# Five blocks of projection columns of an encoder layer, 2560 in all, as seven products of halves instead of eight

## The chip, the cores and the metric

One core of a Trainium2 chip runs the kernel; every time is in device microseconds (us) of that core. PE is TensorE (matmuls), DVE VectorE, ACT ScalarE, POOL GpSimd, and SP SyncE, whose queue issues the DMAs. Lower is better. Before: median 1946.49 us over 3 runs (1945.42 to 1948.09).

## The reference

One layer on a sequence of 1024 tokens, 2048 wide. A normed input is multiplied with one combined weight matrix; its columns are cut into the inputs and gates of four mixers, each gated mixer output is one 512 wide quarter of `y`, and a second matrix brings `y` back.

```python
h = rms_norm(x, norm_g) @ w_in                    # [1024, 2048] @ [2048, 6408]
(a_u, a_v, a_z, b_q, b_k, b_v, b_iq, b_ik, b_iw, b_z,
 c_q, c_kv, c_kr, c_z, d_q, d_k, d_v, d_z) = split_cols(h, IN_SIZES)
y_a = gmlp_mixer(a_u, a_v, ...) * silu(a_z)       # gelu of u and v, spatial mixing
y_b = dsa_mixer(b_q, ..., b_ik, b_iw) * silu(b_z) # index scores, top 256 keys, attention
y_c = mla_mixer(c_q, c_kv, c_kr, ...) * silu(c_z) # attention over low-rank keys
y_d = band_mixer(d_q, d_k, d_v, ...) * silu(d_z)  # attention over nine chunks
x = x + concat([y_a, y_b, y_c, y_d]) @ w_out
```

## The kernel before

**Arithmetic.** Every float32 operand of a large product is cut into a high and a low part (`xh`, `xl`; `wh`, `wl`), and a product is three matmuls: high by high, high by low, low by high. Parts of weights are made by an ACT cast (`wh`, L419) and a POOL subtract (`wl`, L420); parts of activations by an ACT cast and a DVE subtract (`split`, L242 and L243). The normed input, transposed, stays in SBUF as 16 tiles `xh`, `xl` of 128x2048 (tags "th" and "tl", eight each).

**Input projection.** A pass takes 256 columns and all 2048 rows, in eight weight loads of 256 rows. `project` moves 256 weight columns against stationary tokens (matmuls of 256 columns); `project_t` moves 512 tokens against stationary weights (512 columns) and is used where the result is wanted transposed: for the index queries (2 passes), the gates B_Z, D_Z, C_Z, A_Z and the input A_U (2 passes each, ten of twelve). Four PSUM banks are filled in a pass (`banks4`); each is evacuated to a tile of `htile`, a ring of five SBUF tiles called `hs`, and stored to DRAM from there. B_Q, D_K and D_Q are normed on the way: ACT copies the bank (L478) and squares it (L235), DVE norms (L236 to L239), SP stores (L500).

**Order of the work.** PE's program is in the order in which the code issues it. The mixers are generators: a clock in `Driver` counts modelled PE time, `pump` in the projections' loops lets every mixer that is due issue its next piece, so that their short matmuls stand between those of the projections. The other engines are list-scheduled, with `hi_prio` pieces ahead; each engine and SP's one queue then runs its list strictly in order. The top-256 selection is a loop of 31 counting steps: DVE counts five of six row blocks (L700), POOL the sixth (`tq`, L697), ACT sums that (L698). Before, the order of the projections is IQ, B_Q, B_Z, D_V, D_Z, C_Q/C_KV, D_K, D_Q, C_Z, A_V, A_U, A_Z; gates are stored in `sz_d`, and the mixers load them (`z`) and multiply.

**Output.** `w_out` is multiplied as eight units of 512 columns (n=0: groups 1 and 3, n=1: groups 2 and 0), each a product of two by two halves done as seven products (`out_unit`: the Winograd form of Strassen's scheme). `prepare` loads `y` and makes its seven operand halves (A11, S2, S1, S3, A12, A22, S4) in the "th" and "tl" tiles. Results go to PSUM banks X, Y (tag "pp", four), Z ("sc") and are added to `xr`, the residual's tile (L1340 from PSUM, L1348 the first product, from SBUF).

Of the kernel before, what the change touches and what calls it, by code (L numbers as in the profile page):

```python
# [9 lines left out]
F32 = mybir.dt.float32  # L10
# [8 lines left out]
P = 128  # L19
# [116 lines left out]
def build(tc, i, out, dbg=None):  # L136
# [16 lines left out]
    sz_d = dram("sz_d", [2048, SEQ])  # L153
# [237 lines left out]
    hctx, yctx = ExitStack(), ExitStack()  # L391
# [88 lines left out]

    def project_gate(c0, g0):
        for c in range(2):
            def evac(j, hf, ps):
                h = htile()
                with hi_prio():
                    A.activation(h, ps, AF.Tanh, scale=0.5)
                    V.scalar_tensor_tensor(h, h, 1.0, ps, op0=ALU.add, op1=ALU.mult)
                r0 = g0 + 256 * c + P * j
                S.dma_start(sz_d[r0:r0 + P, 512 * hf:512 * hf + 512], h)
            project_t(c0 + 256 * c, evac)  # L490
# [117 lines left out]

    def gate(pl, row, c0, n):
        z = pl.tile([P, n], F32, tag="z", name="z", bufs=1)  # L610
        S.dma_start(z, sz_d[row:row + P, c0:c0 + n])
        return z
# [117 lines left out]
    def b_attention(ap, maskb):  # L730
# [9 lines left out]
        def unit(idx, hp_, b):  # L740
# [26 lines left out]
            if b % 2:  # L767
                po = state["po"]
                row = GB + P * hp_
                z = gate(ap, row, P * (b - 1), 256)  # L770
# [9 lines left out]
                V.tensor_tensor(y, y, z, op=ALU.mult)  # L780
# [23 lines left out]
    def d_attention(ap):  # L804
# [4 lines left out]
        def unit(idx, h, m):  # L809
# [31 lines left out]
            if m % 2:  # L841
# [3 lines left out]
                z = ap.tile([P, 512], F32, tag="z", name="z", bufs=1)  # L845
                S.dma_start(z[r0:r0 + 64], sz_d[row:row + 64, c0:c0 + 512])
# [6 lines left out]
                V.tensor_tensor(y[r0:r0 + 64], y[r0:r0 + 64], z[r0:r0 + 64], op=ALU.mult)  # L853
# [150 lines left out]
    def c_attention(ap):  # L1004
# [11 lines left out]
        def unit(idx, h, b):  # L1016
# [51 lines left out]
            if b % 4 == 3:  # L1068
                state["free"] = drv.t + 1.6
                row, c0 = GC + P * h, P * (b - 3)  # L1070
                z = gate(ap, row, c0, 512)
                y = ap.tile([P, 512], F32, tag="y", name="y", bufs=1)
                V.tensor_tensor(y, state["po"], z, op=ALU.mult)
                S.dma_start(y_d[row:row + P, c0:c0 + 512], y)
# [101 lines left out]
    def gelu2(ps, r):  # L1176
        t, h = r(ttile()), r(htile())
        with hi_prio():
            A.copy(h, ps)
# [7 lines left out]

    project_iq()
# [12 lines left out]
    done.add("dz")  # L1201
    project_gate(C_Z, GC)
    done.add("cz")
# [4 lines left out]
    for c in range(2):  # L1208
        def evac(j, hf, ps):
            r0 = 256 * c + P * j  # L1210
            S.dma_start(ug_d[r0:r0 + P, 512 * hf:512 * hf + 512], gelu2(ps, lambda t: t))
        project_t(A_U + 256 * c, evac)
    done.add("au")
    yp = None
    for c in range(2):
        def evac(j, hf, ps):
            r0, cs = 256 * c + P * j, slice(512 * hf, 512 * hf + 512)
            t = yp.tile([P, 512], F32, tag="ug", name="ug", bufs=4)
            S.dma_start(t, ug_d[r0:r0 + P, cs])
            h = htile()  # L1220
            with hi_prio():
                A.activation(h, ps, AF.Tanh, scale=0.5)
                V.scalar_tensor_tensor(h, h, 1.0, ps, op0=ALU.add, op1=ALU.mult)
                V.tensor_tensor(h, h, t, op=ALU.mult)
            S.dma_start(y_d[GA + r0:GA + r0 + P, cs], h)

        def before():
            nonlocal yp
            if yp is None:
                drv.until(lambda: "am" in done and not drv.threads)  # L1230
                yp = yctx.enter_context(pool("yp"))

        project_t(A_Z + 256 * c, evac, before)
# [8 lines left out]
    A11, S2, S1, S3, A12, A22, S4 = (0, 0), (0, 1), (0, 2), (0, 3), (1, 0), (1, 1), (1, 2)  # L1242
    op = ctx.enter_context(pool("op", side="right"))
    slots = {}

    def split_y(kt, at, src):
        split(slots[kt][at[0]][0][:, at[1]], slots[kt][at[0]][1][:, at[1]], src)

    def load_y(g, kt):
        t = op.tile([P, SEQ], F32, tag="ys", name="ys", bufs=3)  # L1250
        S.dma_start(t, y_d[512 * g + P * kt:512 * g + P * (kt + 1)])
        return t

    def prepare(g1, g2, part):
        for kt in range(4):
            slots.setdefault(kt, {})[part] = (big("th", "yh"), big("tl", "yl"))
            with hi_prio():
                r = load_y(g2, kt)
                a12, a22 = r[:, 0:512], r[:, 512:1024]
                if part == 0:  # L1260
                    q = load_y(g1, kt)
                    a11, a21 = q[:, 0:512], q[:, 512:1024]
                    split_y(kt, A11, a11)
                    V.tensor_tensor(a22, a21, a22, op=ALU.add)
                    V.tensor_tensor(a12, a22, a11, op=ALU.subtract)
                    split_y(kt, S2, a12)
                    split_y(kt, S1, a22)
                    V.tensor_tensor(a21, a11, a21, op=ALU.subtract)
                    split_y(kt, S3, a21)
                else:  # L1270
                    split_y(kt, A12, a12)
                    split_y(kt, A22, a22)
                    for t in slots[kt][0]:
                        V.tensor_tensor(a12, a12, t[:, S2[1]].bitcast(F32), op=ALU.subtract)
# [90 lines left out]
    for n, (g1, g2) in enumerate(((1, 3), (2, 0))):  # L1365
        for part in range(2):
            prepare(g1, g2, part)
# [41 lines left out]
```

## Time and profile before

| what | value |
| --- | --- |
| median of 3 runs | 1946.49 us |
| profiled execution: its own time, its span | 1946.34 us, 1944.5 us |
| mean granted clock of TensorE, share of full speed | 0.993 |
| PE busy | 1884.5 us, 97% of the span |
| DVE, ACT, POOL busy | 60%, 40%, 37% |
| matmuls of 512 columns in the ten passes that change | 1920 |

The span is the stretch from the first to the last instruction that the profiler saw; 1.84 us lie around it. PE's busy time counts modelled ends of pipelined matmuls, so the pitch from start to start is the better price of one.

### The profile page before, as it was taken

The page shows a single profiled execution, that of the slowest core. Times are in us where ns is not written, and L with a number is a line of the kernel's source. Part 1 is how long each engine was busy: PE and PEld are TensorE (multiplying, and loading weights), DVE is VectorE, ACT ScalarE, POOL GpSimd, SP SyncE. Part 2 cuts the span into 40 slices and gives each one's busy share as a digit, 9 for nine tenths or more (in the row PEclk, how much of TensorE's full clock was granted, in tenths as well). Part 3 has the DMA queues.
Part 4 walks back from the last instruction along what each step waited for, and adds up shares of the span by engine and source line. Part 5 has one row for each costly group of instructions (what it writes and reads, how often), then busy time and mean ns, then how long its engine had stood idle before and what let it go on. Part 6 is the DMA issues. An engine that isn't in the chain of part 4 may idle for free.

```text
span 1944.5 us, 34880 instructions
## 1 busy us (share of the span) xinstructions
PE 1884.5 (97%) x13068; PEld 1755.4 (90%) x13068; DVE 1170.0 (60%) x3033; ACT 779.7 (40%) x1565; POOL 716.2 (37%) x784
## 2 busy tenths in 40 slices
PE   5999999999999999999999999999999998998999
PEld 4988998899888999999998889998888888998999
DVE  6514899888366554488745665743343666459644
ACT  6424533332455454344325555644453242224221
POOL 4121256763344443222223333422222233445443
PEclk9999999999999999999999999999999998999999
DMA  7231122222322221433334333243333755546443
GB/s 222 87 109 33 33 66 72 68 69 78 104 82 76 61 66 58 117 121 122 104 107 122 104 108 96 68 135 102 99 98 98 241 198 182 170 152 228 130 144 117
DMA packets 184573, 216.20 MB, mean 111 GB/s; under 512 B 25891, under 2 KB 135636, under 8 KB 184276
## 3 DMA queue, kind: packets, MB, share of 16 engines
q1 hardware_dynamic: 184404, 213.98, 36.0%
q8 instruction: 103, 1.69, 0.4%
q14 instruction: 66, 0.54, 0.1%
HBM read 149.16 MB, written 60.58 MB: 108 GB/s over the span
## 4 chain that ended last, share of the span: by engine, by line
PE 81%; DMA 8%; DVE 6%; issue 2%; SPq 1%; POOL 1%; ACT 1%; DVEq 0%; POOLq 0%; ACTq 0%
PE pp L206 59%; PE sc L206 12%; PE sc L210 5%; PE po L206 5%; DMA out<-xr 2%; DMA duo<-vd_d 1%; DVE yl L243 1%; DMA wr<-in_w_in 1%; DMA ys<-y_d 1%; DMA nat<-qk_d 1%; SPq L302 1%; DMA xr<-pt_d 1%; DMA duo<-qd_d 1%; POOL wl L1287 0%; DVE xr L1340 0%
## 5 line engine op out<-in xcount | busy, mean ns | idle before, releaser
L420 POOL TENSOR_TENSOR wl<-wr,wh 128x512 fp32r<-128x512 f32 x192 | 257.4, 1341 | 523.8 <-ACT wh L419 474.6
L206 PE MATMUL pp<-wh,xh 128*128 128x256 f32 x1536 | 436.9, 284 | 0.0
L206 PE MATMUL pp<-wh,xl 128*128 128x256 f32 x1536 | 433.7, 282 | 0.0
L206 PE MATMUL pp<-wl,xh 128*128 128x256 f32 x1536 | 432.7, 282 | 0.0
L206 PE MATMUL pp<-xh,wh 128*128 128x512 f32 x768 | 309.1, 402 | 0.0
L206 PE MATMUL pp<-xh,wl 128*128 128x512 f32 x768 | 304.3, 396 | 0.0
L206 PE MATMUL pp<-xl,wh 128*128 128x512 f32 x768 | 304.0, 396 | 0.0
L206 PEld LDWEIGHTS pp<-wl,xh 128*128 128x128 f32 x1536 | 290.7, 189 | 1.2
L206 PEld LDWEIGHTS pp<-wh,xh 128*128 128x128 f32 x1536 | 289.9, 189 | 1.2
L206 PEld LDWEIGHTS pp<-wh,xl 128*128 128x128 f32 x1536 | 288.9, 188 | 0.0
L419 ACT CAST wh<-wr 128x512 fp32r<-128x512 f32 x192 | 118.9, 619 | 362.8 <-PE pp L206 314.9
L1287 POOL TENSOR_TENSOR wl<-wo,wh 128x512 fp32r<-128x512 f32 x96 | 138.2, 1440 | 169.1 <-ACT wh L1286 166.6
L206 PE MATMUL pp<-wh,yh 128*128 128x256 f32 x640 | 182.9, 286 | 13.6 <-DVE xr L1340 10.0
L530 POOL TENSOR_SCALAR sS<-sS,den 128x640 f32<-128x640 f32 (+7 forms) x160 | 116.1, 727 | 215.1 <-DVE den L529 156.3
L206 PE MATMUL pp<-wh,yl 128*128 128x256 f32 x640 | 182.9, 286 | 3.5 <-DVE yl L243 3.5
L206 PE MATMUL pp<-wl,yh 128*128 128x256 f32 x640 | 182.0, 284 | 0.0
L206 PEld LDWEIGHTS pp<-xh,wl 128*128 128x128 f32 x768 | 144.5, 188 | 34.9
L206 PEld LDWEIGHTS pp<-xl,wh 128*128 128x128 f32 x768 | 144.9, 189 | 28.9
L206 PEld LDWEIGHTS pp<-xh,wh 128*128 128x128 f32 x768 | 144.7, 188 | 29.1 <-issue 0.3
L528 ACT ACTIVATE sS<-sS,nm 128x640 f32<-128x640 f32 (+7 forms) x160 | 119.0, 744 | 125.2 <-DVE nm L525 110.1
L700 DVE TENSOR_SCALAR_CACHE_REDUCE t<-score,cand 128x896 bf16<-128x896 f32 (+4 forms) x155 | 135.9, 877 | 4.2
L206 PEld LDWEIGHTS pp<-wh,yh 128*128 128x128 f32 x640 | 122.7, 192 | 15.1 <-issue 6.8
(254 smaller groups left out, 3949.6 us busy)
## 6 DMA issues: line engine op xcount, KB each, us to landing
wr<-in_w_in SPq DMA_DIRECT2D x192, 256.0 KB, 2.8
wo<-in_w_out SPq DMA_DIRECT2D x32, 512.0 KB, 3.9
ys<-y_d SPq DMA_DIRECT2D x24, 512.0 KB, 4.2
xt<-in_x SPq DMA_DIRECT2D x32, 256.0 KB, 3.9
xr<-in_x SPq DMA_DIRECT2D x16, 512.0 KB, 5.5
pt_d<-xr SPq DMA_DIRECT2D x16, 512.0 KB, 7.0
xr<-pt_d SPq DMA_DIRECT2D x16, 512.0 KB, 6.1
out<-xr SPq DMA_DIRECT2D x16, 512.0 KB, 7.2
```

What stands on the lines that cost most here:

```text
L206: T.matmul(o, l, r, start=start, stop=stop, skip_group_check=True)
L210: T.transpose(o, t, ident)
L243: V.tensor_tensor(lo, src, hi.bitcast(F32), op=ALU.subtract)
L302: S.dma_start(raw[:, :, o:o + n], rows[:, c0:c0 + n].rearrange("(k p) c -> p k c", p=P))
L419: A.copy(hi, raw)
L420: G.tensor_tensor(lo, raw, hi.bitcast(F32), op=ALU.subtract)
L528: A.activation(sS[:, :tot], sS[:, :tot], AF.Exp, bias=nm[:, 0:1], accum_out=den[:, 0:1])
L530: G.tensor_scalar(sS[:, :tot], sS[:, :tot], den[:, 1:2], 0.5, op0=ALU.mult, op1=ALU.mult)
L700: V.tensor_scalar(t1[:, :n], score[:, SOFF[b]:SOFF[b] + n], th, None, op0=op, op1=ALU.add, accum_out=cnt[:, b - 2:b - 1])
L1287: G.tensor_tensor(lo, src, hi.bitcast(F32), op=ALU.subtract)
```

## The change

The ten passes of `project_t` over A_U and the gates become `half_unit`s. The 2048 rows are taken in two chunks of 1024; within a chunk, tokens, rows and columns are halved (512 tokens, 512 rows, 128 columns) and the two by two product is done as seven products. One product is 4 k-tiles by 3 matmuls of 512 columns, so there are 2 chunks x 10 groups x 7 x 12 = 1680 of them where there were 1920. For that:

- `store_x`, a new generator that runs beside IQ, B_Q and D_V, makes the seven input halves of both chunks: 64 POOL instructions on 128x512 and 56 stores of 256 KB to `xs_d`, through the `htile` ring. `prepare_x` loads seven of 1 MB per chunk and splits them (28 ACT casts, 28 DVE subtracts).
- A unit loads its 1 MB of weights into one buffer `raw` (two DMAs of 512 KB), makes seven operands by four DVE instructions and seven casts and subtracts, and adds results into `acc`. Chunk 0 stores `acc` to `ct_d`; chunk 1 loads it again, adds to it, and applies gelu or the gate.
- The gate multiplies leave the mixers: chunk 1 loads the mixer's `y`, multiplies, and stores it again. The passes stand behind A_V, in the order A_U, B_Z, D_Z, C_Z, A_Z, twice.
- In the output, every operand half has a tile of its own (`renew`), the product with A22 gets two banks `W` ("sc" and "po"), so eight in all; A12 goes ahead of S3, and stores are issued earlier, those of the last unit in parts.

```diff
+    def store_x():
+        yield 30.0
+        for chunk in range(2):
+            for kt in range(4):
...
+                a11, a21 = block(0, 0), block(0, 1)
+                yield 5.0
+                put(A11, a11)
+                t = htile()
+                G.tensor_tensor(t, a11, a21, op=ALU.subtract)
+                put(S3, t)
+                yield 5.0
+                a22 = block(1, 1)
...
+    drv.spawn(store_x())
     project_iq()
     project_heads(B_Q, qb_d, bq_gain)
-    project_gate(B_Z, GB)
     done.add("bq")
     project_heads(D_V, vd_d, None)
-    project_gate(D_Z, GD)
...
+    def prepare_x(chunk):
+        renew(PRODUCTS)
+        with hi_prio():
+            for n, at in enumerate(PRODUCTS):
+                hi, lo = slots[at]
+                S.dma_start(lo.bitcast(F32), xs_d[chunk, n].rearrange("(k p) c -> p k c", p=P))
+                for kt in range(4):
+                    split(hi[:, kt], lo[:, kt], lo[:, kt].bitcast(F32))
...
+    def split_t(src):
+        hi, lo = (wp.tile([P, 4, P], F32R, tag=tag, name=tag, bufs=3) for tag in ("wh", "wl"))
+        A.copy(hi, src)
+        G.tensor_tensor(lo, src, hi.bitcast(F32), op=ALU.subtract)
+        return hi, lo
...
+        a, b, c, d = banks4()
...
+        product(a, A11, "b11", True)
+        p1 = wp.tile([P, 512], F32, tag="wr", name="p1", bufs=2)
+        with hi_prio():
+            A.copy(p1, a)
+            if chunk:
+                for o in (c12, c22, c21):
+                    G.tensor_tensor(o, o, p1, op=ALU.add)
...
+        product(c, S2, "t2", True)
+        add(c12, base(c12), c)
+        product(b, S1, "t1", True)
...
+    for chunk in range(2):
+        prepare_x(chunk)
+        raw = tp.tile([P, 4, 512], F32, tag="tl", name="raw", bufs=8)
+        acc = tp.tile([P, 4, 512], F32, tag="th", name="acc", bufs=8)
+        for n, (c0, evac, need) in enumerate(groups):
+            if chunk:
+                drv.until(lambda: need in done)
+            half_unit(chunk, c0, 256 * n, raw, acc, evac)
...
-        Z = [bank() for _ in range(2)]
+        Z, W = [bank() for _ in range(2)], [bank(), obank()]
...
+        product(X, A12, ws["b21"], False)
+        add(0, 0, X)
         product(Y, S3, ws["t3"], False)
         add(1, 1, Y)
-        product(X, A12, ws["b21"], False)
-        add(0, 0, X)
-        product(Y, A22, ws["t4"], False)
         add(1, 0, Y)
+        product(W, A22, ws["t4"], True)
+        add(1, 0, W)
         product(Z, S4, ws["b22"], False)
```

Three places in the programs of the engines are shown, with what each instruction waits for (DMAHW5 is one of eight counters that landed DMAs raise). First ACT, where the first half of B_Q is evacuated (`hs<-pp` copies of four banks, between counting steps `tq` and weight casts `wh`). Before:

```order
L478 COPY hs_2685<-pp_1927 128x512 [waits PE_49]
L235 ACTIVATE ht_2687<-hs_2685 128x512 [waits Activation_49]
L478 COPY hs_2708<-pp_1928 128x512 [waits PE_49]
L478 COPY hs_2731<-pp_1929 128x512 [waits PE_49]
L235 ACTIVATE ht_2710<-hs_2708 128x512 [waits DVE_49,Activation_49]
L478 COPY hs_2754<-pp_1930 128x512 [waits PE_49]
L419 CAST wh_2901<-wr_2899 128x512 [waits DMAHW2_49]
L698 ACTIVATE tq_2344,cnt_2336<-tq_2344 128x1024 [waits Pool_49]
L235 ACTIVATE ht_2733<-hs_2731 128x512 [waits DVE_49]
L235 ACTIVATE ht_2756<-hs_2754 128x512 [waits DVE_49]
```

and after the change:

```order
L479 COPY hs_2787<-pp_1985 128x512 [waits PE_49]
L236 ACTIVATE ht_2789<-hs_2787 128x512 [waits Activation_49]
L479 COPY hs_2810<-pp_1986 128x512 [waits PE_49]
L479 COPY hs_2833<-pp_1987 128x512 [waits PE_49]
L236 ACTIVATE ht_2812<-hs_2810 128x512 [waits DVE_49,Activation_49]
L420 CAST wh_3012<-wr_3010 128x512 [waits DMAHW2_49,PE_49]
L683 ACTIVATE tq_2424,cnt_2416<-tq_2424 128x1024 [waits Pool_49]
L236 ACTIVATE ht_2835<-hs_2833 128x512 [waits DVE_49]
L683 ACTIVATE tq_2424,cnt_2416<-tq_2424 128x1024 [waits Pool_49]
L479 COPY hs_2856<-pp_1988 128x512 [waits DMAHW5_49,DVE_49]
L236 ACTIVATE ht_2858<-hs_2856 128x512 [waits Activation_49]
```

The fourth copy now stands behind the third square and a counting step, and waits for a DMA (DMAHW5) as well: the ring tile that it gets is that of the first copy, `hs_2787`, whose store has to land. `store_x` holds two of the five ring tiles there. The second half of B_Q reads alike.

Second POOL, in the same stretch, where it alternates between counting steps `tq` and weight subtracts `wl`. Before:

```order
L697 TENSOR_SCALAR tq_2344<-score_1100,cand_2339 128x1024 [waits DVE_49,Activation_49]
L420 TENSOR_TENSOR wl_2966<-wr_2963,wh_2965 128x512 [waits DMAHW3_49,Activation_49,Pool_49]
L420 TENSOR_TENSOR wl_3030<-wr_3027,wh_3029 128x512 [waits DMAHW4_49,Activation_49,Pool_49]
L697 TENSOR_SCALAR tq_2344<-score_1100,cand_2339 128x1024 [waits DVE_49]
L420 TENSOR_TENSOR wl_3094<-wr_3091,wh_3093 128x512 [waits DMAHW5_49,Activation_49,Pool_49]
L697 TENSOR_SCALAR tq_2344<-score_1100,cand_2339 128x1024 [waits DVE_49,Activation_49]
```

and after, with the instructions of `store_x` (`hs<-...`) between them:

```order
L682 TENSOR_SCALAR tq_2424<-score_1101,cand_2419 128x1024 [waits DVE_49,Activation_49] x2
L1198 TENSOR_TENSOR hs_2919<-hs_2630,hs_2628 128x512 [waits DMAHW6_49]
L1182 TENSOR_TENSOR hs_2922<-xh_106,xl_114 128x512 [waits Pool_49]
L421 TENSOR_TENSOR wl_3081<-wr_3078,wh_3080 128x512 [waits DMAHW3_49,Activation_49]
L1204 TENSOR_TENSOR hs_2989<-hs_2922,hs_2919 128x512 [waits Pool_49]
L682 TENSOR_SCALAR tq_2424<-score_1101,cand_2419 128x1024 [waits DVE_49]
L1182 TENSOR_TENSOR hs_3056<-xh_104,xl_112 128x512 [waits DMAHW7_49,Pool_49]
L1182 TENSOR_TENSOR hs_3058<-xh_105,xl_113 128x512 [waits DMAHW0_49]
L421 TENSOR_TENSOR wl_3149<-wr_3146,wh_3148 128x512 [waits DMAHW4_49,Activation_49]
L1189 TENSOR_TENSOR hs_3125<-hs_3056,hs_3058 128x512 [waits DMAHW2_49,Pool_49]
L1182 TENSOR_TENSOR hs_3182<-xh_107,xl_115 128x512 [waits DMAHW3_49,DVE_49]
```

Up to three more instructions of 128x512 now stand between two subtracts. From the first of these rows that `store_x` brought (`hs_2919`) to its last instruction, POOL has 27 of `store_x`, 15 `wl` and 12 `tq`.

Third PE, where the A_V pass (`project`, matmuls of 256) ends. Before, A_U follows, whose weights have long been loaded:

```order
L206 MATMUL pp_11215<-wl_11669,xh_106 128x256
L206 MATMUL pp_11215<-wh_11668,xl_114 128x256
L206 MATMUL pp_11812<-xh_99,wh_11818 128x512 [waits Activation_49]
L206 MATMUL pp_11812<-xl_107,wh_11818 128x512
L206 MATMUL pp_11812<-xh_99,wl_11819 128x512 [waits Pool_49]
```

and after, a few transposes of a mixer (`cn`) and the first half unit (operands called `yh`, `yl` as in the output) follow:

```order
L207 MATMUL pp_10817<-wl_11403,xh_107 128x256
L207 MATMUL pp_10817<-wh_11402,xl_115 128x256
L211 MATMUL sc_11485<-ident_97,cn_11293 128x128 [waits DMAHW0_49,DVE_49,Activation_49]
L211 MATMUL sc_11485<-ident_97,cn_11293 128x128 x2
L211 MATMUL sc_11485<-ident_97,cn_11293 128x128 [waits DVE_49]
L207 MATMUL pp_11644<-yh_11530,wh_11612 128x512 [waits Activation_49]
L207 MATMUL pp_11644<-yl_11531,wh_11612 128x512 [waits DMAHW4_49]
L207 MATMUL pp_11644<-yh_11530,wl_11613 128x512 [waits Pool_49]
```

and SP's queue ahead of that unit:

```order
L1276 DMA yl_11539<-xs_d_59 128x4x512 [waits DMAHW4_49,PE_49]
L1276 DMA yl_11541<-xs_d_59 128x4x512 [waits DMAHW5_49,PE_49]
L1276 DMA yl_11543<-xs_d_59 128x4x512 [waits DMAHW6_49,PE_49]
L977 DMA qk_d_68<-qk_11172 128x1536 [waits DMAHW7_49,DVE_49]
L1293 DMA raw_11607<-in_w_in 128x4x256 [waits PE_49]
L1293 DMA raw_11607<-in_w_in 128x4x256 [waits DMAHW1_49]
```

The weights `raw` of the first half unit wait for PE, since their tile is that of the last `xl`, which the last A_V matmuls read; its cast and first matmul follow from there.

## Rows read from the trace of the kernel before

**Rows 1.** The page: span, then busy time (share) of each engine.
```profile
span 1944.5 us, 34880 instructions
...
PE 1884.5 (97%) x13068; PEld 1755.4 (90%) x13068; DVE 1170.0 (60%) x3033; ACT 779.7 (40%) x1565; POOL 716.2 (37%) x784
```

**Rows 2.** Busy time by stretch: length, then each engine (its instructions), clock, DMA.
```profile
core 0: us, PE busy (x) PEld busy (x) DVE busy (x) ACT busy (x) POOL busy (x), PEclk, DMA share, GB/s
306.40:396.40 90.00, 90.00 (x387) 72.36 (x385) 81.57 (x235) 29.82 (x54) 58.51 (x30) 1.00 0.26 78
396.40:488.50 92.10, 92.10 (x769) 92.10 (x768) 73.14 (x153) 22.98 (x40) 46.83 (x28) 1.00 0.26 74
1610.00:1770.00 160.00, 151.57 (x1237) 151.11 (x1237) 91.67 (x124) 43.33 (x73) 70.79 (x52) 0.97 0.52 172
1770.00:1944.00 174.00, 162.57 (x1335) 161.53 (x1334) 98.46 (x134) 46.65 (x78) 79.68 (x55) 0.98 0.45 151
```

**Rows 3.** The page, costliest groups of instructions.
```profile
L420 POOL TENSOR_TENSOR wl<-wr,wh 128x512 fp32r<-128x512 f32 x192 | 257.4, 1341 | 523.8 <-ACT wh L419 474.6
...
L206 PE MATMUL pp<-xh,wh 128*128 128x512 f32 x768 | 309.1, 402 | 0.0
...
L419 ACT CAST wh<-wr 128x512 fp32r<-128x512 f32 x192 | 118.9, 619 | 362.8 <-PE pp L206 314.9
```

**Rows 4.** Waits of PE, 1585 to 1650 us: total, times, longest.
```profile
PE pp L206 <- DVE xr L1340: 8.4, 2, 5.9
```

**Rows 5.** Waits of PE, 1745 to 1800 us.
```profile
PE pp L206 <- DVE yl L243: 3.5, 1, 3.5
PE pp L206 <- ACT yh L242: 2.2, 1, 2.2
```

**Rows 6.** Instructions of ACT in order, 256 to 307.3 us: start, length.
```profile
256.25 0.58 ACT L478 COPY hs<-pp 128x512 f32<-128x512 f32 x1
...
260.56 0.59 ACT L478 COPY hs<-pp 128x512 f32<-128x512 f32 x1
...
302.32 0.59 ACT L478 COPY hs<-pp 128x512 f32<-128x512 f32 x1 [0.82 <-PE pp L206]
```

**Rows 7.** Instructions of DVE in order, 272 to 317.5 us.
```profile
272.41 0.68 DVE L239 TENSOR_TENSOR hs<-hs,bq_gain 128x512 f32<-128x512 f32 x1
...
316.79 0.68 DVE L239 TENSOR_TENSOR hs<-hs,bq_gain 128x512 f32<-128x512 f32 x1
```

**Rows 8.** Tile qb_d, 250 to 345 us: its stores, first and last start.
```profile
L500 SPq DMA_DIRECT2D qb_d<-hs x8: 366/366/367, 273.1 to 333.1; - x8
...
DMA to landing us min/median/max: 2.1/2.6/3.1
```

**Rows 9.** The page, DMA issues: count, KB of each, median us to landing.
```profile
wr<-in_w_in SPq DMA_DIRECT2D x192, 256.0 KB, 2.8
wo<-in_w_out SPq DMA_DIRECT2D x32, 512.0 KB, 3.9
...
pt_d<-xr SPq DMA_DIRECT2D x16, 512.0 KB, 7.0
xr<-pt_d SPq DMA_DIRECT2D x16, 512.0 KB, 6.1
out<-xr SPq DMA_DIRECT2D x16, 512.0 KB, 7.2
```

**Rows 10.** Groups of DVE, 1600 to 1944 us.
```profile
L1340 DVE TENSOR_TENSOR xr<-xr,pp 128x512 f32<-128x512 f32 x64 | 43.0, 682 | 67.0 <-PE pp L206 66.2
L1348 DVE TENSOR_TENSOR xr<-xr,p 128x512 f32<-128x512 f32 x48 | 37.9, 819 | 44.4 <-DMA xr<-in_x 15.1 <-DMA xr<-pt_d 13.9 <-ACT p L1345 11.2
L243 DVE TENSOR_TENSOR yl<-ys,yh 128x512 fp32r<-128x512 f32 x38 | 34.3, 930 | 1.3 <-ACT yh L242 1.3
```

**Rows 11.** Groups of POOL, 306.4 to 396.4 us: busy us, mean ns | idle before.
```profile
L697 POOL TENSOR_SCALAR tq<-score,cand 128x1024 bf16<-128x1024 f32 x14 | 40.1, 2864 | 19.8 <-DVE cand L710 15.8 <-DVE rsr L222 4.0
```

More of the change, by code (lines that the diff above doesn't have):

```diff
@@ L1207, in build @@
         project(A_V + 256 * c, evac)
[L1208 to L1233, printed above, removed]
@@ L1242, in build @@
-    A11, S2, S1, S3, A12, A22, S4 = (0, 0), (0, 1), (0, 2), (0, 3), (1, 0), (1, 1), (1, 2)
-    op = ctx.enter_context(pool("op", side="right"))
     slots = {}
     def split_y(kt, at, src):
[L1247 to L1262, printed above, removed]
+        split(*(t[:, kt] for t in slots[at]), src)
@@ L1263, in prepare, with renew @@
+    def renew(ats):
+        for at in ats:
+            slots[at] = (big("th", "yh"), big("tl", "yl"))
+    def prepare(load, part):
+        renew((S3, A22, S4) if part else (A11, S2, S1, A12))
+        with hi_prio():
+            if part == 0:
+                for kt in range(4):
+                    a11, a21 = load(0, kt)
+                    a12, a22 = load(1, kt)
                     split_y(kt, A11, a11)
                     V.tensor_tensor(a22, a21, a22, op=ALU.add)
-                    V.tensor_tensor(a12, a22, a11, op=ALU.subtract)
@@ new lines, in prepare @@
+            for kt in range(4):
+                a11, a21 = load(0, kt)
+                V.tensor_tensor(a11, a11, a21, op=ALU.subtract)
+                split_y(kt, S3, a11)
+            for kt in range(4):
+                a12, a22 = load(1, kt)
+                split_y(kt, A22, a22)
+                V.tensor_tensor(a12, a12, a22, op=ALU.subtract)
+                for t in slots[S3]:
+                    V.tensor_tensor(a12, a12, t[:, kt].bitcast(F32), op=ALU.add)
+                split_y(kt, S4, a12)
@@ L1277, in load_wo, with load_y, load @@
+    drv.until(lambda: not drv.threads)
+    op = ctx.enter_context(pool("op", side="right"))
+    def load_y(gs):
+        def load(k, kt):
+            t = op.tile([P, SEQ], F32, tag="ys", name="ys", bufs=3)
+            S.dma_start(t, y_d[512 * gs[k] + P * kt:512 * gs[k] + P * (kt + 1)])
+            return t[:, 0:512], t[:, 512:1024]
+        return load
     def load_wo(g, h, c0):
@@ L1372, in build @@
         for c in range(4):
-            out_unit(g1, g2, 512 * c, x_d if n == 0 else pt_d, pt_d if n == 0 else out, rp)
+            out_unit(g1, g2, 512 * c, x_d if n == 0 else pt_d, pt_d if n == 0 else out, rp, n == 1 and c == 3)
     if dbg is not None:
```

181 lines of the change are left out of this document (136 added, 45 removed).

## Prediction

> **What bounds the kernel now.** The page's head comes first: PE is busy for 1884.5 of 1944.5 us, the next engine for 60% [rows 1]. So nearly every matmul that goes is time that goes, unless a wait takes its place. The price of a matmul is read from a stretch in which PE has no gap. From 306.4 to 396.4 us PE is busy all 90.00 us with 387 matmuls, 384 of them the two passes B_Z, three short ones of the neighbours: (90.0 - 3 x 0.12) / 384 = 0.2335 us for 512 columns. From 396.4 to 488.5 us, two passes of 256 columns, it is 92.1 / 769 = 0.12 us, and 5.76 us for each of 16 weight loads [rows 2]. The mean of 402 ns that the page gives for one matmul of 512 columns is its modelled, overlapping length [rows 3] and no price. Where PE does wait is read from the stretches and then from its waits: the two output stretches leave 8.4 and 11.4 us idle [rows 2]. Into the output (1585 to 1650 us) it waits 8.4 us for the add into `xr` [rows 4], between its halves 3.5 and 2.2 us for `yl` and `yh` [rows 5].
>
> **The matmuls removed.** 1920 - 1680 = 240 of 512 columns at 0.2335 us: **-56.0 us**. The clock was 1.00 in the stretch that gives the price, 0.97 and 0.98 in the output stretches [rows 2], so no more is to be had from it.
>
> **The ring in B_Q.** In before, ACT copies the first bank at 256.25 and the fourth at 260.56 us [rows 6]; the next pass fills the banks in the same order and spacing, 4.3 us for three quarters of a round, and so wants the fourth bank free at about 260.6 + 4.3 = 264.9 us. It was, since five ring tiles served four copies. After the change `store_x` holds two of the five, and the order shows that the fourth copy waits for the store of the first one's tile. That tile's last norm instruction runs from 272.41 for 0.68 us [rows 7], the store is issued at 273.1 for 0.37 us and lands after 2.1 to 3.1, mostly 2.6 us [rows 8]. So the fourth copy (0.59 us) ends at about 273.1 + 2.6 + 0.6 = 276.3, and PE loses 276.3 - 264.9 = 11.4 us. The second half: first copy 302.32 us [rows 6], bank wanted 8.7 us later at 311.0, norm ends at 317.5 [rows 7], copy ends at 320.7: 9.7 us. Together **+21 us**. Bounds: landings of 2.1 give 20; the 7.0 us of the slowest store that I see, `pt_d` [rows 9], 30. What is queued behind the waiting copy on ACT: weight casts, of which three are done ahead, and the sums of the counting steps, so the selection is held up with PE and not against it. Nothing else in DVE's norm order is moved. D_V has no norm; its tiles are stored at once, and I cost it at nothing: copy 0.59, issue 0.37 and landing 3.1 are 4.1 us against the 8.7 available.
>
> **Two starts with no weights.** The first unit's `raw` sits in a tile that the last A_V matmul still reads. From there: issue 0.37 [rows 8], landing of 512 KB 3.9 (`wo`, the same load from a weight matrix [rows 9]), cast 0.62, subtract 1.34 [rows 3], less the two matmuls that can run before the low part is wanted, 0.47: 5.8 us. Chunk 1 has the same in front of it, since its `raw` gets the tile of chunk 0's last operand, S4: **+11.6 us**. Below: landing 2.8 as for half the size, 9.4 together; above: 7.2 as for `out` [rows 9], 18.2. Before the change neither place had a wait. Seven loads of 1 MB stand ahead of each start, but take tiles that come free earlier, one per quarter of A_V's last pass or per 2.8 us product.
>
> The Trainium skill, "DMA: Bandwidth & Descriptors", section "Anatomy of one DMA — SWDGE (gpsimd) path", fits a transfer as about 2.0 us plus its bytes at 436 GB/s, for descriptors made by GpSimd; an estimate by it for 512 KB is 3.2 us. Row `wo` has 3.9 us on SP's queue [rows 9], so the measurement decides; by the page the two starts would cost 1.4 us less and the margin below would double, which would make the whole sum about 1920.
>
> **Twenty units in a row.** A unit of nothing but its own matmuls is 84 x 0.2335 = 19.6 us, a product 2.8. Load on the others in chunk 1: POOL 7 subtracts and 3 adds at 1.34 = 13.4 us; ACT 7 casts at 0.62, a copy and 4 tanh near 0.6 = 7.4; DVE 4 + 7 + 8 instructions at 0.68 = 12.9, and more beside POOL: `yl` takes 930 ns in the mean in the output, adds from PSUM 682 [rows 10], so 12 of the 19 with 0.25 to 0.4 us more, 18 at most. All fit, none by much. The chain that is close is the weights': `raw` is one buffer, its last operand (b22) can be split only when the fourth product frees its place among three, after which come cast 0.62, subtract 1.34, issue 0.37, landing 3.9, cast 0.62, subtract 1.34 = 8.2 us. PE has three products and two matmuls, 8.9 us. A margin of 0.7 us, with POOL's three adds and SP's stores in the same queues: I take half a us of wait per unit, **+10 us**, between nothing and 20 (a landing 1.7 us longer).
>
> **POOL beside the selection.** The selection's counting steps stand 14 in 90 us, 6.4 us apart, and `tq` takes 2.86 us of each [rows 11]. From `hs_2919` to the end of `store_x` POOL has 12 x 2.86 + 15 x 1.34 + 27 x 1.34 = 91 us to do, while PE works 15 x 5.76 = 86 us and 12 steps take 77. That alone would cost 5 us, but the ring's 21 us of standing PE lie in it. **+3 us**, from 0 to 15 (by the pitches of the matmuls ahead of it, the attention on the selected keys comes due within 3 us of where it did, so a late mask would be waited for).
>
> **Output.** The operands' splits stay the queue ahead of the first adds into `xr`, about as long: I keep the 8.4 us and the rest of that start. Between the halves each operand tile is free as soon as its own product of the last unit is done, which takes away the 5.7 us: **-5 us**, from -10 (eight banks spare the first adds too) to +10 (POOL 71 of 160 us busy [rows 2], so more slowed DVE splits in a row). The split stores at the end: nothing or half a us.
>
> **Gates.** The multiplies and `z` loads that leave the mixers were off the path; the y loads and stores of chunk 1 lie in DVE's 12.9 us and SP's queue.
>
> **Sum.** 1946.3 (the profiled execution, 0.1 under the median) - 56.0 + 21 + 11.6 + 10 + 3 - 5 = **1931 us**, with single ends of -1, -2, -10, -3, -5 and +9, +7, +10, +12, +15.
>
> **Rivals.**
> (a) The waits are hidden: the ring's tile comes early enough, or the weights' chain has more margin than I see. Without the ring's 21 us: 1910; without the unit waits too: 1900. For it: five tiles with short stores always did in before. Against it: the order names the wait, and the norm that it waits for ended 8 us after the bank was wanted.
> (b) Slower: `raw` lands late in every unit. SP's queue carries 3 MB of loads and 1 MB of stores per unit of chunk 1, and a store that waits for DVE holds the loads behind it. With 6.1 us as for `xr` from `pt_d` [rows 9] a unit waits 1.5 us: 30 in place of 10, 1951 us; with 7.2 us 2.6, and 1973. It decides from a landing of 5.9 us (1.3 us per unit). For it: DMAs of that size take that long in the output stretch; against it: `wo`, in the same stretch, takes 3.9.
> (c) No gain: the starts, the selection and the output each at their upper ends, 1943 to 1950, a sum of middling costs.
>
> **How the numbers follow.** A measurement here tells 0.2%, 3.9 us, from no change. My forecast, 1914 to 1942: 0.52. (a), below 1914: 0.18. (c): 0.12. (b): 0.18, half of it below 1957. Faster 0.70, same 0.12, slower 0.18. Leaving out the lower half of (a) and the upper half of (b) gives 1906 to 1957.
>
> **What would show it.** PE's matmuls fewer by 240 of 512 columns at an unchanged pitch; two gaps of PE of about 10 us in B_Q, ended by the ACT copy of the fourth bank, itself released by a DMA; a gap of some 6 us behind A_V and one between the chunks, ended by ACT's cast of `raw`; gaps under a us between units; no 5.7 us between the output's halves. I am wrong if PE runs through B_Q, or if the gaps between units reach 1.3 us.

## The result, and the profile after

The changed kernel takes 2083.36 us in the median (2080.99 to 2091.71, 4 runs) where the kernel before takes 1947.24 on the same chips: a ratio of 1.0691, 95% interval 1.067 to 1.0712. It is 136 us slower; I had forecast 1931 us. The profiled execution, 2091.71 us, is the longest of the four, 8 us over their median.

The page of the changed kernel: span, busy times, granted clock in 40 slices, one of its DMA issues.

```profile
span 2089.9 us, 35390 instructions
...
PE 1894.5 (91%) x12828; PEld 1750.7 (84%) x12828; DVE 1435.1 (69%) x3307; ACT 855.6 (41%) x1711; POOL 943.8 (45%) x938
...
PEclk9999999999999999999989998989997998999999
...
raw<-in_w_in SPq DMA_DIRECT2D x40, 512.0 KB, 4.4
```

Against [rows 1] the span is 145.4 us longer. PE has the 240 matmuls less that were to go (12828 for 13068), but its busy time is 10 us longer and its idle time went from 60 to 195 us. So 145.4 = -56 (matmuls) + 135 (idle) + 66 (busy time beyond the 1828.5 us that were to be left). A good half of the last, 37.5 us as counted below, is the clock, which was granted at 0.959 of full speed in the mean and at 0.993 before; the rest I have not divided. How idle time and clock hang together shows at the first long stop of PE in the projections, 9.7 us in B_Q. The waits of PE from 250 to 350 us (total, times, longest), the copy on ACT that ended the stop, itself released by a store of the ring (`qb_d<-hs`), five of PE's matmuls behind the stop, and two stretches there with the granted clock (PEclk):

```profile
PE pp L207 <- ACT hs L479: 18.8, 3, 9.7
```

```profile
283.93 0.59 ACT L479 COPY hs<-pp 128x512 f32<-128x512 f32 x1 [4.28 <-DMA qb_d<-hs]
```

```profile
284.56 0.58 PE L207 MATMUL pp<-wh,xh 128*128 128x256 f32 x1 [9.67 <-ACT hs L479]
...
285.16 0.41 PE L207 MATMUL pp<-wh,xl 128*128 128x256 f32 x1
...
287.29 0.41 PE L207 MATMUL pp<-wh,xh 128*128 128x256 f32 x1
...
287.80 0.28 PE L207 MATMUL pp<-wh,xh 128*128 128x256 f32 x1
287.92 0.28 PE L207 MATMUL pp<-wl,xh 128*128 128x256 f32 x1
```

```profile
core 0: us, PE busy (x) PEld busy (x) DVE busy (x) ACT busy (x) POOL busy (x), PEclk, DMA share, GB/s
284.60:287.40 2.80, 2.80 (x13) 2.80 (x14) 2.80 (x8) 1.72 (x3) 2.80 (x2) 0.50 0.06 23
287.70:290.70 3.00, 3.00 (x28) 3.00 (x27) 3.00 (x9) 0.45 (x1) 3.00 (x3) 1.00 0.45 175
```

From 284.56 to about 287.5 us a matmul of 256 columns comes every 0.214 us, at a granted clock of 0.50 (1.2 GHz), then every 0.12, at 1.00 (2.4 GHz). I counted in both traces the runs of four matmuls or more at near twice their pitch: 9 of them before, 38 after, and what they lose is 8.5 and 46 us. Of the changed kernel's 46 stops of over a us, 36 have such a run within 8 us behind them, of the 17 before, 7. A run mostly adds 1 to 2.5 us to the price of its stop.

To see where the time goes I took from every start-to-start distance of PE the pitch of its matmul at full clock (0.234 us for 512 columns, 0.12 for 256) and summed the rest by stretch:

| stretch | lost before, us | lost after, us |
| --- | --- | --- |
| up to IQ | 18.6 | 17.1 |
| IQ, B_Q, D_V | about 0 | 31.6 |
| from there to the first unit | about 0 | 24.8 |
| the mixers D, C and A, with passes (before) or units (after) | 21 | 140 |
| output | 20 | 43 |

The units' 758 us hold more than half of the loss (140 of 257 us), and 119 of the 197 us that it grew by. The stretch, then its last four units by themselves, which no mixer stands beside, and then PE's longer waits in the first sixteen:

```profile
core 0: us, PE busy (x) PEld busy (x) DVE busy (x) ACT busy (x) POOL busy (x), PEclk, DMA share, GB/s
959.20:1717.20 758.00, 668.18 (x3447) 563.39 (x3448) 523.62 (x1230) 349.52 (x721) 333.08 (x388) 0.93 0.48 147
1622.40:1717.20 94.80, 84.33 (x337) 65.87 (x336) 69.78 (x81) 32.52 (x56) 58.34 (x40) 0.95 0.65 216
```

```profile
PE pp L207 <- ACT wh L1282: 14.5, 3, 7.4
PE sc L207 <- DVE vt L1112: 9.9, 3, 5.4
PE pp L207 <- DVE acc L1326: 9.9, 1, 9.9
PE sc L207 <- DMA krl<-krl: 8.8, 3, 3.5
PE po L207 <- ACT ph L243: 6.2, 4, 2.2
PE sc L207 <- DVE rst L222: 5.3, 1, 5.3
PE sc L211 <- DMA ws<-in_a_ws: 5.1, 1, 5.1
```

Four kinds stand here: weights not ready (`wh`, L1282), 11.8 of the 14.5 us where a chunk begins; `acc`, the units' sums; loads for the mixers that land late (`krl`, `ws`); and links of the mixers' chains (`vt`, `ph`, `rst`). The four units without mixers take 94.8 us where 336 matmuls at 0.234 are 78.6, so they lose 16 us, 4 each; 9.2 of them are waits for `acc`:

```profile
PE pp L207 <- DVE acc L1326: 9.2, 3, 5.1
```

In its first output unit PE waits 9.6 us for a cast `yh` and 8.5 in all for `yl`; the kernel before waited there for `xr` instead, 8.4 us [rows 4]. Between the output's halves the waits for `yl` and `yh` [rows 5] are gone, and one of 5.3 us for `xr` stands in their place. The waits of the whole output stage:

```profile
PE sc L207 <- ACT yh L243: 9.6, 1, 9.6
PE pp L207 <- DVE yl L244: 8.5, 3, 4.4
PE pp L207 <- DVE xr L1468: 6.8, 2, 5.3
```

### The profile page after: what moved, and what is told of

It is laid out like the page before. It is cut to its first block, busy times and chain, and to the rows that moved or that the text cites. A ratio compares the mean times of both kernels' runs of the same rounds, so it can differ in the third digit from the quotient of the medians.

```text
span 2089.9 us, 35390 instructions
## 1 busy us (share of the span) xinstructions
PE 1894.5 (91%) x12828; PEld 1750.7 (84%) x12828; DVE 1435.1 (69%) x3307; ACT 855.6 (41%) x1711; POOL 943.8 (45%) x938
## 5 line engine op out<-in xcount | busy, mean ns | idle before, releaser
L207 PE MATMUL pp<-wh,xh 128*128 128x256 f32 x1536 | 437.6, 285 | 18.8 <-ACT hs L479 18.8
L207 PE MATMUL pp<-yh,wh 128*128 128x512 f32 x560 | 238.8, 426 | 34.0 <-DVE acc L1326 19.1
L1283 POOL TENSOR_TENSOR wl<-raw,wh 128x512 fp32r<-128x512 f32 x120 | 164.4, 1373 | 193.9 <-ACT wh L1282 178.3
L421 POOL TENSOR_TENSOR wl<-wr,wh 128x512 fp32r<-128x512 f32 x112 | 152.1, 1358 | 212.5 <-ACT wh L420 177.8
L207 PE MATMUL pp<-yh,wl 128*128 128x512 f32 x560 | 231.2, 413 | 3.4 <-POOL wl L1283 3.2
L207 PE MATMUL pp<-yl,wh 128*128 128x512 f32 x560 | 230.5, 412 | 0.0
L207 PEld LDWEIGHTS pp<-yh,wh 128*128 128x128 f32 x560 | 112.2, 200 | 57.8 <-ACT wh L1282 23.7
L207 PE MATMUL pp<-wh,yh 128*128 128x256 f32 x512 | 148.1, 289 | 8.8 <-DVE xr L1468 6.8
L420 ACT CAST wh<-wr 128x512 fp32r<-128x512 f32 x112 | 69.3, 619 | 196.8 <-PE pp L207 142.0
L207 PEld LDWEIGHTS pp<-yh,wl 128*128 128x128 f32 x560 | 111.1, 198 | 33.0 <-POOL wl L1283 5.9
L207 PEld LDWEIGHTS pp<-yl,wh 128*128 128x128 f32 x560 | 112.0, 200 | 20.9
```

Of the source, the lines that this page charges most:

```text
L207: T.matmul(o, l, r, start=start, stop=stop, skip_group_check=True)
L420: A.copy(hi, raw)
L421: G.tensor_tensor(lo, raw, hi.bitcast(F32), op=ALU.subtract)
L1283: G.tensor_tensor(lo, src, hi.bitcast(F32), op=ALU.subtract)
```

## The experiments

I compare each kernel's ratio to the kernel before with the 1.0691 of the changed kernel, and give differences in us of 1947. The 95% intervals of the ratios are 2 to 8 us to either side, and 4 for the changed kernel's own, so a difference of a few us shows nothing. Where nothing else is said an edit is on the changed kernel.

**The parts by themselves.** First the output stage on the kernel before (the diff's part from `slots` on, nothing else).

> The kernel before with the rearranged output stage alone (a tile per operand, eight banks, A12 ahead of S3). Theory: the output edit is worth what I forecast, and the 20 us that the output stages lose in the changed kernel come from inputs that arrive late behind the half units: 1940 to 1946 us, the 5.7 us between the output's halves gone. Rival: the rearranged output itself makes the waits (its splits stand in other places of DVE's queue): 1958 to 1970 us.

1953.89 us, ratio 1.002 (1.0008 to 1.0032), +4 us. Neither: the wait between the halves is not gone, it is now for adds into `xr` that stand behind the splits in DVE's queue.

```profile
PE pp L206 <- DVE xr L1350: 14.1, 3, 5.4
PE pp L206 <- POOL wl L1297: 2.7, 3, 1.5
```

In before that add cost 8.4 us at the output's start [rows 4], and `yl` and `yh` 5.7 between the halves [rows 5]. By the sum of the table above this kernel's output loses 7 us more than that of before, so some 7 of the 23 us more that the changed kernel loses there are the output's own.

Then `store_x` on the kernel before, started ahead of IQ as in the changed kernel, its results unread.

```diff
+    drv.spawn(store_x())
     project_iq()
     project_heads(B_Q, qb_d, bq_gain)
     project_gate(B_Z, GB)
```

> The kernel before, with store_x added and its seven halves never read. Theory: the price of making them is that of the ring and of IQ, 25 to 35 us above before, 1973 to 1983 us, with two waits of PE for the copies of B_Q's fourth bank near 10 us each. Rival: with B_Z between B_Q and D_V there is room, and it costs less than 10 us.

1982.24 us, ratio 1.0172 (1.0156 to 1.0187), +33 us, with the waits in B_Q and IQ:

```profile
PE pp L207 <- ACT hs L479: 19.0, 3, 9.7
PE sc L207 <- ACT rl L670: 4.7, 9, 0.9
PE pp L207 <- DVE hs L488: 3.3, 1, 3.3
```

And the order alone: ten passes of `project_t` behind A_V, gates applied there, no seven products.

```diff
+    for n, (c0, evac, need) in enumerate(groups):
+        project_t(c0, evac, lambda: drv.until(lambda: need in done))
```

> The kernel before, with only the order of the change: its ten passes of project_t stand behind A_V in the changed kernel's order, gates applied there to the mixers' stored results, no seven products, no store_x, output as before. Theory: the work of the units on DVE, POOL, ACT and SP costs most; the move by itself costs the 25 us that the changed kernel loses between B_Q and the first unit, where mixers now stand beside normed passes, and at most 10 elsewhere: 1965 to 1985 us. Rival: the move itself breaks the cover of the mixers and most of the loss is here: over 2010 us.

1984.55 us, ratio 1.0184 (1.0163 to 1.0204), +36 us. In before the attention on selected keys starts beside D_Z and D attention beside C_Z, gate passes with nothing to norm; with those gone the first stands beside C_Q and D_K, and the low-rank mixer (`cn`) beside A_V. The waits, 540 to 1640 us:

```profile
PE sc L211 <- DVE cn L914: 6.3, 1, 6.3
PE sc L211 <- issue: 4.9, 1, 4.9
PE sc L211 <- DMA gs<-bd_r: 4.5, 1, 4.5
PE po L207 <- DVE pl L244: 4.4, 8, 2.1
PE sc L211 <- DMA duo<-qd_d: 4.0, 1, 4.0
```

By the sum of the table, this kernel loses 20 us between D_V and its ten passes and 39 us beside the mixers, where before lost about 0 and 21. So the order by itself makes most of what the changed kernel loses ahead of its first unit, and some 18 us of the 119 more in the units' stretch.

If the parts add, of +136, +36 is the order, +33 is `store_x`, -56 the matmuls; some 120 are left for the units and what they do to the output.

**The ring and POOL.** `store_x` does a whole block in one step, so that no ring tile is held between steps:

```diff
-                yield 5.0
...
+                yield 25.0
```

> The changed kernel, with store_x doing each of its eight blocks in one step, so that it holds no ring tile while B_Q is evacuated. Theory: the two waits of PE for the copy of B_Q's fourth bank (9.8 and 8.5 us) and the slow clock behind each go: 2083 - 22, about 2061 us. Rival: POOL, not the ring, is what holds this stretch; its instructions now come eight at a time, weights come late, and nothing is gained: 2078 to 2088 us.

2079.57 us, ratio 1.0661 (1.0645 to 1.0677), -6 us, at the edge of the uncertainty. The wait at 274 us was gone, and one of 11 us at 319 us took its place: the second pass's first copies on ACT are released by an instruction of `store_x` on POOL (L1195), which still reads a ring tile.

```profile
329.47 1.07 ACT L479 COPY hs<-pp 128x512 f32<-128x512 f32 x2 [2.52 <-POOL hs L1195]
```

Then `store_x` starts behind B_Q:

```diff
-        yield 30.0
+        yield lambda: "bq" in done
```

> The changed kernel, with store_x starting only when B_Q's passes are issued, beside D_V, whose tiles are stored without a norm. Theory of the ring: both waits in B_Q go and none takes their place, and IQ's waits for relu tiles (5 us in all) go too, since POOL and SP are as before there: 20 to 30 us less, 2054 to 2063 us. Rival: store_x is as much in the way wherever it runs, as with the eight blocks in one step, which moved the wait to the next evacuation: 2075 to 2083 us.

2087.59 us, ratio 1.0707 (1.0665 to 1.0749): no gain. The ring's waits and IQ's are gone, and one of 32.6 us stands at 497 us, before the attention on selected keys:

```profile
PE sc L211 <- DMA duo<-kn_d: 32.6, 1, 32.6
```

The load of `kn_d` stands behind the making of the masks (it is issued right behind the last mask in all three kernels, at 478, 496 and 527 us), and the counting steps show why those came late. POOL's step in the kernel before, in the changed one, and here (31 of them, first and last start):

```profile
L697 POOL TENSOR_SCALAR tq<-score,cand x31: 2841/2844/3134, 239.7 to 439.9; 128x1024 bf16<-128x1024 f32 x31
```

```profile
L682 POOL TENSOR_SCALAR tq<-score,cand x31: 2832/2842/3336, 249.8 to 457.3; 128x1024 bf16<-128x1024 f32 x31
```

```profile
L682 POOL TENSOR_SCALAR tq<-score,cand x31: 2842/2845/3135, 239.0 to 480.1; 128x1024 bf16<-128x1024 f32 x31
```

30 intervals take 200, 207 and 241 us: 6.7, 6.9 and 8.0 us each. It is not POOL's own queue that sets them in e5_pause: POOL is busy for 202 of these 241 us, DVE for 222, and POOL's steps still wait 16 us for `cand` from DVE. The time is in the three short DVE instructions of a step, on six elements. In the kernel before, and here:

```profile
L714 DVE COPY_PREDICATED R<-mi,cand 128x6 int32<-128x6 int32 x30 | 8.2, 274 | 0.8
L713 DVE TENSOR_SCALAR mi<-cnt 128x6 int32<-128x6 f32 x30 | 6.3, 209 | 9.6 <-ACT tq L698 7.6 <-DVE rsr L222 0.3
L710 DVE TENSOR_SCALAR cand<-R 128x6 int32<-128x6 int32 x30 | 5.1, 171 | 2.9 <-DVE R L714 0.5
```

```profile
L699 DVE COPY_PREDICATED R<-mi,cand 128x6 int32<-128x6 int32 x30 | 23.8, 792 | 0.8
L695 DVE TENSOR_SCALAR cand<-R 128x6 int32<-128x6 int32 x30 | 18.7, 623 | 2.5
L698 DVE TENSOR_SCALAR mi<-cnt 128x6 int32<-128x6 f32 x30 | 17.3, 578 | 12.1 <-ACT tq L683 10.1 <-DVE rsr L223 0.3
```

They sum to 19.6 and 59.8 us, 40 of the 41 us that the steps take longer. In e5_pause `cand` takes 0.17 us where no POOL instruction overlaps it (15 times) and 1.08 us in the mean where one does (16 times). So `store_x` holds the selection up by keeping POOL running while DVE has these to do; in the changed kernel, whose ring stops PE there, the three sum to 37 us and the steps take 7 us longer than before. Behind the selection both are gone:

```diff
-        yield 30.0
+        yield lambda: "cq" in done
```

> The changed kernel, with store_x starting only when C_Q's passes are issued, behind the selection, beside D_K and D_Q. In e5_pause the counting steps went from 6.7 to 8.0 us each and the masks came 33 us late. Theory: the changed kernel has two limits there at once, the ring (18 us of waits in B_Q) and POOL beside the selection, and each hides the other; clear of both, IQ and B_Q lose nothing, and D_K and D_Q little, since their norms don't queue behind counts: 20 to 30 us less, 2055 to 2065 us. Rival: SP's one queue is the limit, and 56 more stores on it hold mixers and weights wherever they run: 2075 to 2085 us.

2056.41 us, ratio 1.055 (1.0525 to 1.0575), -27 us, and the waits of PE from 100 to 350 us are gone. Of the kernels with the whole change it is the shortest, and still 107 us above before.

**The units.** Chunk 1 starts its sums anew, which leaves chunk 0's sums out of the result:

```diff
-                    S.dma_start(acc[:, 2 * t + n], ct_d[rows[n], 512 * t:512 * t + 512])
...
-                for o in (c12, c22, c21):
-                    G.tensor_tensor(o, o, p1, op=ALU.add)
```

> The changed kernel, in which chunk 1 starts its sums anew (leaves out the load of chunk 0's sums and POOL's three adds of the first product). Theory of the single buffer acc: a unit of chunk 1 can't load its sums before the unit ahead has stored its results, and PE waits for the add at the end of that chain; without the load 25 to 35 us less, some 2052 us. Rival: the waits of chunk 1 come from the queues of DVE, ACT and POOL being full; no more than 8 us less.

2053.37 us, ratio 1.0527 (1.0511 to 1.0543), -32 us. The chain it removes, at the 9.9 us wait of the changed kernel (DVE, SP, POOL, DVE in order of time):

```profile
1368.00 0.69 DVE L1166 SCALAR_TENSOR_TENSOR acc<-ht,acc 128x512 f32<-128x512 f32 x1 [0.69 <-ACT ht L1165]
1368.72 0.32 SPq L1372 DMA_DIRECT2D ug_d<-acc  x1
1371.10 1.26 POOL L1334 TENSOR_TENSOR acc<-acc,p 128x512 f32<-128x512 f32 x1 [4.34 <-DMA acc<-ct_d]
1372.39 0.69 DVE L1326 TENSOR_TENSOR acc<-acc,pp 128x512 f32<-128x512 f32 x1 [3.70 <-POOL acc L1334]
```

Gelu writes its result into `acc`; the store to `ug_d` must land before the next unit's sums are loaded into the same place; POOL's add waits for that load, DVE's for POOL, and a bank for DVE's. The edit takes more away than the chain, though: 40 loads on SP's queue and 30 adds on POOL. PE's own waits for `acc` sum to 19 us in the changed kernel (9.9 and 9.2 above). An attempt to be rid of the chain and leave nothing out, on top of e5_pause: chunk 0's sums are added at the end, from a ring tile.

```diff
+                s = htile()
+                S.dma_start(s, ct_d[rows[n], ts])
+                V.tensor_tensor(s, s, o, op=ALU.add)
+                evac(s, P * n, ts)
```

> The kernel of e5_pause, in which chunk 1 sums its own products as chunk 0 does and adds chunk 0's sums at the end, from a ring tile of their own (nothing is left out; POOL's three adds go, DVE gets four more per unit). Theory of the single buffer: the chain store, load, add is off the banks, so most of the 30 us of e3_no_reload come again: 20 to 30 us under e5_pause. Rival: DVE has no room for four more instructions, or the five ring tiles serve three uses per result and become the wait: no more than 8 us under e5_pause, or above it.

2084.13 us, ratio 1.0685 (1.0642 to 1.0728), 4 us under e5_pause, inside the uncertainty. PE's waits for `acc` are down from 17.5 us to 2.5, but DVE has four more instructions a unit, and other waits took the place.

Next, all side work of a unit is left out but four bank copies, one weight load per chunk and the stores of the A groups:

> The changed kernel, in which the half units leave out everything but their matmuls in order, four copies of banks by ACT, one weight load per chunk, and stores of the A groups (no weight loads, splits, combinations, adds, partial sums, gates). Theory: the waits beside the mixers come from the work that units put on DVE, POOL, ACT and SP; of 140 us lost from the first unit to the last less than 30 stay: about 1960 to 1975 us. Rival: the mixers' pieces are issued too close together for their own latencies, now that fewer matmuls stand between them; 60 us or more stay: over 2000 us.

1971.67 us, ratio 1.0116 (1.008 to 1.0151), -112 us. The same stretch, with 3446 matmuls for 3447, to be laid beside that of the changed kernel above:

```profile
956.60:1608.80 652.20, 632.48 (x3446) 538.99 (x3447) 293.01 (x944) 274.54 (x590) 106.51 (x224) 0.99 0.31 92
```

652 us for 758, at a clock of 0.99 for 0.93, DVE busy 293 for 524 us and POOL 107 for 333. So the order and density of the mixers' pieces on PE is not what stops it; the units' side work is. By the sum of the table 35 of the 140 us stay in the stretch, a little over the 30 that I named and near the 39 that e10_move loses there. Parts of the side work, in three kernels, with `split_t` returning `hi, hi` and the four `V.tensor_tensor` lines of `half_unit` taken out:

```diff
-        G.tensor_tensor(lo, src, hi.bitcast(F32), op=ALU.subtract)
-        return hi, lo
+        return hi, hi
...
-            V.tensor_tensor(b11, b12, b11, op=ALU.subtract)
-            V.tensor_tensor(t2, b22, b11, op=ALU.subtract)
```

both:

> The changed kernel, in which the half units leave out the low parts of their weights (POOL's seven subtracts; PE multiplies with the high part twice) and DVE's four combinations of weights. Theory of load: the mixers beside the units wait because the units fill POOL and DVE: 40 us or more less, under 2045 us, in the stretches of D and C attention above all. Rival: the waits come from the order on SP's queue and from the chain through acc, which stay: at most 12 us less.

only the first:

> The changed kernel, in which the half units leave out only POOL's seven subtracts (PE multiplies with the high part twice), and keep DVE's four combinations. e4_thin left out both and was 50 us shorter. Theory: POOL's queue is the larger part, since it also carries the mixers' normalisation and the three adds ahead of which they stand: 30 us or more less, under 2055 us. Rival: DVE, the busier engine, is what the mixers wait for: 20 us less or fewer, over 2063 us.

only the second:

> The changed kernel, in which the units leave out only DVE's four combinations of weights (the low parts are made). Theory: the parts of e4_thin add, so DVE's 80 instructions are worth the 50 - 21 = 29 us that e12_no_low left: 2050 to 2058 us. Rival: each alone frees the weights' chain and they overlap: 2035 to 2045 us, or they are worth something only together: over 2068 us.

2033.39 us (1.0425, 1.0399 to 1.0451), 2062.42 (1.0579, 1.0557 to 1.0602) and 2040.78 (1.0486, 1.0464 to 1.0509): -52, -22 and -40 us. The two make 62 us by their sum and 52 together, an overlap that is hardly clear of the uncertainty of some 5 us in each: DVE's 80 instructions, 0.7 to 1.1 us each, are worth 40 us by themselves, POOL's 140 are worth 22, and 12 more once DVE's are gone. The combinations are also links of the weights' chain, and no run tells that from their load on DVE. DVE rows of the changed kernel in the units' stretch show how the two meet:

```profile
L1326 DVE TENSOR_TENSOR acc<-acc,pp 128x512 f32<-128x512 f32 x98 | 65.8, 681 | 44.8 <-PE pp L207 35.5 <-POOL acc L1334 7.9 <-PE sc L211 1.1
...
L1365 DVE SCALAR_TENSOR_TENSOR hs<-hs,acc 128x512 f32<-128x512 f32 x29 | 27.1, 933 | 9.6 <-ACT hs L1364 9.4
...
L1366 DVE TENSOR_TENSOR hs<-hs 128x512 f32<-128x512 f32 x28 | 24.3, 869 | 0.4
...
L1304 DVE TENSOR_TENSOR raw<-raw,t 128x512 f32<-128x512 f32 x20 | 22.0, 1098 | 6.9 <-POOL wl L1283 6.9
```

An add with one operand in PSUM takes 681 ns. Of the instructions of the same size with both operands in SBUF, these take 0.87 to 1.1 us in the mean, and three others of a unit 0.70. The means mix two cases: the last combination (L1304) takes 0.68 us where no POOL instruction overlaps it (9 of 20) and 1.44 in the mean where one does, the add from PSUM 0.68 either way. The Trainium skill ("SBUF — State Buffer", section "Who interferes with whom") says that a DVE instruction with two SBUF inputs contends with a GpSimd instruction that reads SBUF; these rows agree. In e12_no_low, without POOL's subtracts, the gates' multiply (L1366 here) falls from 869 to 722 ns in the mean; the last combination (L1304) falls only from 1.10 to 1.01 us. There the eight that run beside POOL's adds of the first product still take 1.35 to 1.78 us, the other twelve 0.68 to 0.80.

The last gate, whose store and loads stand ahead of the output's in SP's queue, is left out:

> The changed kernel, in which the last unit leaves out its gate (no tanh, no load of gelu(u)): its sums are stored directly. Theory of SP's queue: the loads of y for the output stand behind loads and stores of the last gates, which wait for DVE; without them the first output unit's 30 us of waiting fall to the 14 of e1_output_alone, 2067 us or so. Rival: the wait is DVE's own queue of splits, which start late because the operand tiles come free late: at most 6 us less.

2071.48 us, ratio 1.0629 (1.0591 to 1.0666), -12 us, between the two: the first output unit lost 22 us where it had lost 30.

The gates of B, D and C are left out:

> The changed kernel, in which units 13 to 18 leave out the gates of B, D and C (no load of y, no tanh, no two DVE instructions, no store; the mixers' results stay ungated). Theory of load: 48 DVE instructions, 24 of ACT and 48 DMAs less in the stretch where C attention and the spatial mixing run: 15 to 30 us less, 2053 to 2068 us. Rival: the gates are behind the path as in the kernel before: under 8 us.

2069.02 us (2058.8 to 2076.84), ratio 1.0618 (1.058 to 1.0656), -14 us, at the edge of what I called load. Do these parts add? e9_late, e3_no_reload and e4_thin in one kernel, and then without those gates as well:

> The changed kernel with e9_late, e3_no_reload and e4_thin together (left out: the load of chunk 0's sums, the low parts of the units' weights and their combinations). Alone they were 27, 30 and 50 us. Theory that they are separate limits: 107 us less, about 1976 us. Rival: one wait hides another as in e5_pause, and together they give much less: over 1995 us.

> The kernel of e13_three, which also leaves out the gates of B, D and C. Theory: what then stays above e8_bare without its store_x loss (1972 - 27 = 1945 us) is DVE's seven adds a unit and the weight loads; 1950 to 1965 us. Rival: the gates cost only while the rest fills DVE; as e13_three, within 4 us.

1989.35 us (1.0206, 1.0189 to 1.0223) and 1979.57 (1.0161, 1.0141 to 1.0181): -94 us where the parts sum to 111, and 9 more. They are separate limits for the most part; the sixth by which they fall short is what they hide of each other. Both misses are of size: I had named 1976 and 1950 to 1965.

## Why the prediction was wrong, step by step

**The matmuls removed**: right, 240 at the forecast pitch. "No more is to be had" from the clock missed that the clock could be lost: 38 us more of slow matmuls behind stops, no term of the sum.

**The ring in B_Q**: right, 11.4 and 9.7 us forecast, 18.8 us found in three waits, the longest 9.7, ended by the copy that a store released, as forecast. **POOL beside the selection**: right that the ring's stops cover it; I gave it 3 us, and e5_pause shows one wait of 33 when it is uncovered. The mechanism was another than the one I summed: not POOL's work against PE's, but DVE's short instructions, each up to a us longer beside POOL. Not foreseen was IQ, 10 us, beside `store_x`'s first instructions.

**Two starts with no weights**: right, both ended by the cast of `raw`. The sum, 11.6 us forecast and 11.8 found, is in part luck: I had 5.8 for each, and found 7.4 and 4.4.

**Twenty units in a row**: the step that failed, +10 us for what lost 140 where before lost 21 in the same place (some 18 of the difference is the order's, e10_move). Of its own mechanism, `raw` late in the steady state, one wait of 2.7 us for `wh` and 3 us in all for `wl` are to be seen; the load took 4.4 us in the median, near the 3.9 I took. Even the four units with nothing but their own matmuls lose 4 us each where I gave half a us. What I did not look at: (1) the second single buffer, `acc`, whose reuse goes over DRAM: 19 us of PE's waits; leaving it out with POOL's adds and the loads gives 32 (e3_no_reload), and e6_fix, which keeps the sums, gives nothing that is clear of the uncertainty. (2) The mixers. I summed each engine's work in a unit of nothing but its own matmuls and found that it fits; but 16 of 20 units, which lose some 124 of the 140 us, stand beside mixers whose chains go from PE to DVE, ACT or POOL and back, and need those engines at once, not in the mean. DVE's share in the stretch of these mixers rose from 53% (317 of 593 us before) to 69%. e8_bare, which takes all of it away, gives 112 us, e4_thin 52. **Rival (b)**, slower, had the right sign and the wrong place.

**The move**: costed at nothing beyond the gates; 36 us (e10_move). The passes taken away were those beside which the mixers made PE lose next to nothing; why the others cover them less was not tried apart. (The PE rows shown ahead of the prediction as A_V's end in the kernel before are those of D_Q's end, where C_Z follows; A_V's end, 297 us later, reads alike, and no number rested on it.) **Gates**: called off the path; 14 us, give or take 8 (e15_no_gate), 9 with DVE freed.

**Output**: -5 us forecast; +4 by itself (e1_output_alone), and 23 more lost in place, of which 8 go with the last gate. The waits for `yl` and `yh` between the halves are gone as forecast, but one of 5.3 us for an add into `xr` took their place: the limit there is DVE's order of adds and splits, which I took to be as before.

The sum of the parts, 1947 - 56 + 36 + 33 + 4, is 1964 us; the 119 us that remain are the units' and what they do to the output. e8_bare, without the side work, gives back 112 of them; the three parts and the gates of e16_four, less the 27 us that belong to `store_x`, 76. That the side work is the cause is shown; how the remainder divides between DVE's seven adds a unit, the splits where a chunk begins and SP's queue was not tried apart.

## What to carry to other kernels

When PE is busy for 97%, a cut in matmuls is paid out only if what replaces them stays off the queues that PE's other users wait in: price the side work by the chains that share its engines, not by whether each engine's sum fits into the stretch. List every single buffer of a new loop and follow its reuse, through DRAM if it goes there. And when two waits stand in one place, expect that removing one shows the other.

## What the runs showed of the hardware

A stop of PE costs more than its length: behind the one of 9.7 us some 3 us of matmuls ran at 1.2 GHz (granted clock 0.50), and over the kernel such stretches lost 46 us where before had 8.5. No kernel here fills a stop with other matmuls, so what would keep the clock is left open.

DVE's short instructions can be held up by POOL for several times their length: in e5_pause three on six elements took 0.17 us each alone and 0.75 to 1.16 us in the mean beside a POOL instruction, which made a step of the selection 8.0 us long where it had been 6.7.
